# Kurtosis of 1024 rows on one core: a first load in two pieces, three groups loaded as whole rows, and dummy matmuls before the first transposes

## The chip, the cores and the metric

The kernel runs on one core of one Trainium2 chip. The metric is the device time in microseconds (us) of one execution; lower is better. Times are given as the median of several executions with the lowest and the highest. The profile's span is some 1.8 us shorter than the time (95.2 us against 97.0 us for the kernel before), and all moments below are counted from the start of the span.

## The reference

```
def reference(x):                       # x: 1024 x 8192, float32
    mean = np.mean(x, axis=-1, keepdims=True)
    std = np.std(x, axis=-1, keepdims=True)
    z = (x - mean) / (std + 1e-8)
    return (np.mean(z ** 4, axis=-1) - 3).astype(np.float32)
```

The input is 33.55 MB and is read once. Each row needs its mean first, then the sum of squares and the sum of fourth powers of the centred values.

## The kernel before

The 1024 rows are worked through in 16 groups of 64 rows. A row lies on two partitions, so that a group is a tile of 128 partitions and 4096 columns. Five such tiles are held at a time. For each group the list says in which pieces its columns are loaded, how many columns of the fourth power ScalarE takes (VectorE takes the rest), and which engine forms the mean.

```
GROUPS = [
    (2, [4096], 1280, 'DVE'),
    ...
    (2, [4096], 1536, 'DVE'),               # group 3
    (2, [2304, 1792], 640, 'PE'),           # group 4, the first with transposes
    ...
    (2, [1536, 1280, 768, 512], 1760, 'both'),   # group 15
]
```

All loads go through one queue, one transfer for a piece:

```
def load(i):
    ...
    for w in pieces:
        nc.sync.dma_start(out=xt[:, c:c + w], in_=src[:, c:c + w])
        c += w
```

Groups 0 to 3 get their mean from one VectorE instruction that adds the two halves of the whole tile, and a matmul. Groups 4 to 14 get it from 32 transposes on TensorE that add up in PSUM (`tps`), a reduction on VectorE (`red`) and a matmul (`mps`). ScalarE copies the result (`nmu`) and squares the tile with it as bias:

```
def mean(i):
    if engine == "DVE":
        nc.tensor.matmul(mps, lhsT=blk[k], rhs=added_halves(i, 0), start=True, stop=True)
    ...
    else:
        tps = transposed_sums(i, n_cols // k)        # 32 transposes of 128 x 128
        nc.tensor.matmul(mps, lhsT=pair_sums(tps), rhs=negcol, start=True, stop=True)
    nc.scalar.copy(nmu, mps)

def keep_busy(n):                                    # the dummies; used at the tail already
    for _ in range(n):
        nc.tensor.matmul(idle, lhsT=zeros[:, :P], rhs=zeros, start=True, stop=True)

for i in range(L):
    mean(i)
    square(i)                                        # ScalarE
    if i >= 1:
        fourth_dve(i - 1, GROUPS[i - 1][2])          # VectorE
        load_next(i - 1)                             # the tile of group i-1 is free
    ...
    fourth_act(i, 0, GROUPS[i][2])                   # ScalarE
```

## Time and profile before

| | before |
|---|---|
| time, 6 runs | 97.08 us (97.00 to 97.14) |
| span of the profile | 95.2 us |
| busy: TensorE, VectorE, ScalarE | 62%, 76%, 84% |
| DMA, mean over the span | 353 GB/s, 433 GB/s from 10 to 15 us |
| first load: issued, wanted data there | 0.80, 8.6 us |

The busy shares say little here, since they are averages. What counts are the two rows of digits in which hardly a slice is below 9 (ScalarE and DMA), and the places where one of the two is seen to wait for the other. The prediction shows these lines.

### The profile page before, as it was taken

To read this page: it belongs to the slowest core of one execution; us is meant where nothing else is said; L and a number is where in the kernel's file an instruction comes from. 1 tells how busy PE (TensorE), PEld (TensorE's weight loads), DVE (VectorE), ACT (ScalarE), POOL (GpSimd) and SP (SyncE) were. 2 spreads that over 40 slices of the span, in tenths; PEclk is the share of its full clock that TensorE was granted. 3 is DMA by queue.
4 is the path that set the end of the run, shared out by engine and by line. 5 is a ranking of instruction groups with operands and counts; after the bars stand their busy time and mean duration, and the time that the engine had idled before them with its cause. 6 is when DMAs were issued, how large, how long until landed. Compare 5 with 4: busy or idle time off the path is not lost.

```text
span 95.2 us, 1248 instructions
## 1 busy us (share of the span) xinstructions
PE 59.5 (62%) x450; PEld 52.5 (55%) x450; DVE 72.7 (76%) x63; ACT 79.8 (84%) x88; POOL 2.7 (3%) x12
## 2 busy tenths in 40 slices
PE   0000202001089797979796969797979797989770
PEld 0000202001089696969695959686969696874330
DVE  2003529999995294979797979897999698999970
ACT  6000099999999779999999999999999999999970
POOL 6400000000000000000000000000000000000000
PEclk9999999999999999999999999999999999999999
DMA  4799999999999999999999999999999999700000
GB/s 89 268 433 433 433 427 433 440 433 394 425 429 413 425 428 429 412 422 412 433 409 430 424 419 420 415 408 403 423 412 420 416 407 408 276 15 0 0 0 1
DMA packets 4789, 33.63 MB, mean 353 GB/s; under 512 B 560, under 2 KB 560, under 8 KB 3248
## 3 DMA queue, kind: packets, MB, share of 16 engines
q1 hardware_dynamic: 4784, 33.56, 85.6%
q8 instruction: 3, 0.05, 0.2%
q14 instruction: 2, 0.02, 0.1%
HBM read 33.55 MB, written 0.00 MB: 352 GB/s over the span
## 4 chain that ended last, share of the span: by engine, by line
PE 26%; DMA 24%; ACT 18%; DVE 18%; issue 11%; SPq 0%; DVEq 0%
DMA xt<-in_x_dram 24%; PE tps L138 21%; ACT xt L182 16%; DVE xt L194 7%; DVE junk L155 7%; DVE red L144 2%; PE mps L174 2%; ACT xt L189 1%; PE pk L240 1%; PE mps L165 1%; PE pf L232 1%; SPq L132 0%; ACT nmu L176 0%; DVE q L194 0%; PE p L222 0%
## 5 line engine op out<-in xcount | busy, mean ns | idle before, releaser
L182 ACT ACTIVATE xt<-xt,nmu 128x4096 f32<-128x4096 f32 (+1 forms) x17 | 59.8, 3516 | 0.5
L194 DVE CUSTOM_DVE_ANT_0 xt<-xt 128x3456 f32<-128x3456 f32 (+8 forms) x17 | 57.5, 3386 | 2.3 <-ACT xt L182 1.9
L138 PE MATMUL tps<-ident,xt 128*128 128x128 f32 x380 | 46.9, 282 | 0.5 <-DMA xt<-in_x_dram 0.5
L138 PEld LDWEIGHTS tps<-ident,xt 128*128 128x128 f32 x380 | 43.9, 147 | 1.8 <-DMA xt<-in_x_dram 0.9
L165 PE MATMUL mps<-part,blk 128*128 128x1 f32 x8 | 2.3, 351 | 24.8 <-DVE part L155 24.8
L155 DVE CUSTOM_DVE_ANT_0 junk<-xt 128x2048 bf16<-128x2048 f32 (+1 forms) x5 | 9.6, 1915 | 9.9 <-DMA xt<-in_x_dram 9.9
L165 PEld LDWEIGHTS mps<-part,blk 128*128 128x128 f32 x8 | 2.0, 311 | 25.0 <-issue 11.0
L189 ACT ACTIVATE xt<-xt 128x640 f32<-128x640 f32 (+7 forms) x16 | 13.9, 870 | 0.5
L176 ACT COPY nmu<-mps 128x1 f32<-128x1 f32 x16 | 2.4, 148 | 10.7 <-PE mps L165 9.4
L144 DVE TENSOR_REDUCE red<-tps 128x128 f32<-128x256 f32 x12 | 5.1, 424 | 6.7 <-PE tps L138 6.6
L174 PEld LDWEIGHTS mps<-negcol,red 128*128 128x128 f32 x22 | 3.3, 188 | 8.9 <-issue 3.3
L174 PE MATMUL mps<-negcol,red 128*128 128x1 f32 x22 | 3.9, 249 | 6.5 <-DVE red L144 5.3
L203 PE MATMUL idle<-zeros 128*128 128x512 f32 x10 | 4.8, 609 | 0.0
L182 ACT ACTIVATION_READ_ACCUMULATOR xt<-xt,nmu 128x1 f32 x17 | 3.1, 184 | 0.0
L189 ACT ACTIVATION_READ_ACCUMULATOR xt<-xt 128x1 f32 x16 | 3.0, 186 | 0.0
L203 PEld LDWEIGHTS idle<-zeros 128*128 128x128 f32 x10 | 1.7, 191 | 1.4 <-issue 1.4
L67 ACT ACT_TABLE_LOAD x1 | 1.3, 1283 | 0.8 <-PEq L301 0.8
L194 DVE DVE_READ_ACCUMULATOR2_ANT q<- 128x1 f32 x17 | 1.4, 83 | 0.0
L218 PEld LDWEIGHTS p<-s,blk 128*128 128x128 f32 x4 | 0.7, 189 | 1.2 <-ACT xt L182 0.7
L66 DVE MEMSET zeros<- 128x512 f32 x1 | 0.5, 485 | 1.0 <-PEq L301 1.0
L218 PE MATMUL p<-s,blk 128*128 128x1 f32 x4 | 0.7, 234 | 0.7 <-ACT xt L182 0.7
L240 PE MATMUL pk<-blk,q 128*5 128x64 f32 (+1 forms) x10 | 1.0, 219 | 0.0
(32 smaller groups left out, 10.5 us busy)
## 6 DMA issues: line engine op xcount, KB each, us to landing
xt<-in_x_dram SPq DMA_DIRECT2D x8, 1152.0 KB, 11.4
xt<-in_x_dram SPq DMA_DIRECT2D x4, 2048.0 KB, 14.5
xt<-in_x_dram SPq DMA_DIRECT2D x8, 896.0 KB, 13.3
xt<-in_x_dram SPq DMA_DIRECT2D x7, 768.0 KB, 11.1
xt<-in_x_dram SPq DMA_DIRECT2D x3, 512.0 KB, 12.5
xt<-in_x_dram SPq DMA_DIRECT2D x1, 640.0 KB, 12.0
xt<-in_x_dram SPq DMA_DIRECT2D x1, 384.0 KB, 12.4
xt<-in_x_dram SPq DMA_DIRECT2D x1, 256.0 KB, 11.3
```

Source lines behind the costliest of these rows:

```text
L138: nc.tensor.matmul(tps, lhsT=xts[i][:, c:c + P], rhs=ident, start=c == 0, stop=c == w - P, is_transpose=True)
L144: nc.vector.tensor_reduce(out=red.rearrange("p (r k) -> p r k", k=2), in_=tps.rearrange("p (r k) -> p r k", k=2).unsqueeze(2).to_broadcast ...
L155: nc.vector.tensor_tensor_reduce(out=junk[:, :h], in0=t[:, :h], in1=t[:, h:], scale=1.0, scalar=0.0, op0=AO.add, op1=AO.add, accum_out=part)
L165: nc.tensor.matmul(mps, lhsT=blk[k], rhs=added_halves(i, 0), start=True, stop=True)
L174: nc.tensor.matmul(mps, lhsT=pair_sums(tps), rhs=negcol, start=True, stop=True)
L176: nc.scalar.copy(nmu, mps)
L182: nc.scalar.activation(out=t, in_=t, func=AF.Square, bias=nmus[i], accum_out=s2[:, j + second:j + second + 1])
L189: nc.scalar.activation(out=t, in_=t, func=AF.Square, accum_out=quads[0][:, j:j + 1])
L194: nc.vector.tensor_tensor_reduce(out=t, in0=t, in1=t, scale=1.0, scalar=0.0, op0=AO.mult, op1=AO.add, accum_out=quads[1 + second][:, j:j + 1])
L203: nc.tensor.matmul(idle, lhsT=zeros[:, :P], rhs=zeros, start=True, stop=True)
L218: nc.tensor.matmul(p2[:, n - 1:], lhsT=blk[k], rhs=s2[:, n - 1 + j:n + j], start=j == 0, stop=j == 1)
L240: nc.tensor.matmul(pk, lhsT=t, rhs=m, start=j == 0, stop=j == len(terms) - 1)
```

## The change

Its intent, as the few words given with it and the code let one read it: fewer transfers for the groups whose columns need not be there early, the clock of TensorE raised before the first transposes so that they take 3.7 and not 5.9 us, and a first load whose first part is small. The columns of ScalarE for groups 4 to 7 are lowered to go with it.

```
 GROUPS = [
-    (2, [4096], 1280, 'DVE'),
+    (2, [1024, 3072], 1280, 'DVE'),
     ...
-    (2, [2304, 1792], 640, 'PE'),      # groups 4, 5, 6: three such lines
+    (2, [4096], 576, 'PE'),
-    (2, [2304, 1792], 640, 'PE'),      # group 7
+    (2, [2304, 1792], 512, 'PE'),
 ...
+    FIRST = [g[3] for g in GROUPS].index("PE")      # 4
     ...
     for i in range(L):
+        if i == FIRST - 1:
+            keep_busy(4)
         mean(i)
```

More of the change, by code (lines that the diff above doesn't have):

```diff
@@ L20 @@
     (2, [4096], 1536, 'DVE'),
-    (2, [2304, 1792], 640, 'PE'),
-    (2, [2304, 1792], 640, 'PE'),
-    (2, [2304, 1792], 640, 'PE'),
-    (2, [2304, 1792], 640, 'PE'),
+    (2, [4096], 576, 'PE'),
+    (2, [4096], 576, 'PE'),
+    (2, [4096], 576, 'PE'),
+    (2, [2304, 1792], 512, 'PE'),
     (2, [2304, 1792], 512, 'PE'),
```

## The prediction

> **What bounds the kernel now.** I read the page first (busy shares, the slices, the chain), then the timeline from 8 us to the end, then the waits, then the busy time in short stretches. The slices come first; each digit is a fortieth of the 95.2 us span, 2.38 us.
>
> ```profile
> ACT  6000099999999779999999999999999999999970
> ...
> PEclk9999999999999999999999999999999999999999
> DMA  4799999999999999999999999999999999700000
> GB/s 89 268 433 433 433 427 433 440 433 394 425 429 413 425 428 429 412 422 412 433 409 430 424 419 420 415 408 403 423 412 420 416 407 408 276 15 0 0 0 1
> ```
>
> The reader is to see two resources without slack. The DMA engines are full from slice 3 to slice 34, and ScalarE from slice 6 on, with one dip in slices 14 and 15 (31 to 36 us). PEclk shows only what the throttle grants. It does not show whether TensorE has warmed up.
>
> The dip is explained by the timeline from 21 to 34 us (start, duration, engine, line, operation, in brackets the idle time before it and who ended it):
>
> ```profile
> 21.30 0.56 PE L165 MATMUL mps<-part,blk 128*128 128x1 f32 x2 [4.73 <-DVE part L155]
> ...
> 26.53 0.56 PE L165 MATMUL mps<-part,blk 128*128 128x1 f32 x2 [4.67 <-DVE part L155]
> ...
> 26.95 5.87 PE L138 MATMUL tps<-ident,xt 128*128 128x128 f32 x32
> ...
> 27.12 0.16 ACT L176 COPY nmu<-mps 128x1 f32<-128x1 f32 x1
> ...
> 32.85 0.42 DVE L144 TENSOR_REDUCE red<-tps 128x128 f32<-128x256 f32 x1 [2.92 <-PE tps L138]
> ...
> 33.64 3.69 PE L138 MATMUL tps<-ident,xt 128*128 128x128 f32 x32
> 33.81 0.16 ACT L176 COPY nmu<-mps 128x1 f32<-128x1 f32 x1 [1.09 <-PE mps L174]
> ```
>
> The first 32 transposes (group 4) take 5.87 us, the next 32 (group 5) 3.69 us. ScalarE needs the mean of group 4 and waits 1.09 us for it. That is its only long idle time after it starts. The stretches of 0.25 us (length, busy and number of transposes that begin, clock granted, DMA share, GB/s) show the first set going slowly, then fast:
>
> ```profile
> 29.00:29.25 0.25, 0.25 (x3) 1.00 1.07 442
> ...
> 31.75:32.00 0.25, 0.25 (x5) 1.00 1.03 430
> ```
>
> What carries from there to the end is in the timeline at 64 to 67 us, group 11:
>
> ```profile
> 64.18 1.51 PEld L138 LDWEIGHTS tps<-ident,xt 128*128 128x128 f32 x14 [0.15 <-DMA xt<-in_x_dram]
> ...
> 65.97 0.42 DVE L144 TENSOR_REDUCE red<-tps 128x128 f32<-128x256 f32 x1 [0.57 <-PE tps L138]
> ...
> 66.54 0.35 PE L174 MATMUL mps<-negcol,red 128*128 128x1 f32 x2 [0.61 <-DVE red L144]
> 66.68 0.19 ACT L189 ACTIVATION_READ_ACCUMULATOR xt<-xt 128x1 f32 x1
> ...
> 66.93 0.16 ACT L176 COPY nmu<-mps 128x1 f32<-128x1 f32 x1
> ```
>
> The second piece of group 11 arrives at 64.18 and TensorE is waiting for it. Its mean is ready at 66.89, and ScalarE is free at 66.87. **Two chains meet here to within 0.02 us**: arrivals through TensorE, and ScalarE's own work since 33.81. From here TensorE's chain of transposes, reduction and mean goes on at about 4.8 us a group to the mean of group 14 (ready at 81.37, ScalarE free at 81.29), and the tail of some 11 us is fixed. So a gain on only one of the chains is lost at group 11. The end moves by roughly the smaller of the two gains.
>
> **What the Trainium skill says.** "TensorE: Matmul & The Clock Gate", Part 1 (the HAM clock gate): the array runs at half clock until one activity window of about 3.4 us has been busy, and the window runs freely, so the moment depends on its phase. The trace agrees: TensorE becomes busy at 26.53 and speeds up at about 31.5, 5 us later. The same page, Part 4 (PE-mode transpose), says that transposes do not count as busy in the same way, so that full clock is not reached. This trace differs: the speed changes in the middle of nothing but transposes. "DMA: Bandwidth & Descriptors", section Bandwidth, puts the fabric ceiling at 435 GB/s. The trace agrees with 433 GB/s in the stretch from 10 to 15 us, where each row goes as one packet, and has 421 from 30 to 40 us, where a row goes in two.
>
> **The change part by part.**
>
> *Whole rows for groups 4 to 6.* A group is 128 x 4096 x 4 bytes, 2.10 MB: at 433 GB/s 4.84 us, at 421 GB/s 4.98 us. Each transfer saved is thus worth about 0.1 to 0.14 us of DMA time. Three are saved, 0.3 to 0.4 us. The price is that transposes of a group wait for all of it. Group 1 landed at 13.49; with three more groups at about 4.86, group 4 lands whole near 28.0, group 5 near 33, group 6 near 37.9. Before, their transposes began at 26.95, 33.64 and 38.15. So only group 4's must begin later, by about 1 us, and once TensorE is warm that is harmless: 28.1 + 3.7 + 0.05 + 0.44 + 0.14 + 0.37 puts its mean at 32.8, a microsecond before the 33.8 of now.
>
> *First group in two pieces.* The mean of group 0 is one VectorE instruction over halves of the whole row, so nothing can use the first 1024 columns early. The extra transfer costs 0.1 to 0.14 us. The ramp of the queue may change: in slices 1 and 2 it moves 89 and 268 GB/s, and the first load lands 7.8 us after issue, of which 4.84 us is transfer. Smaller first packets could shorten the ramp or lengthen it; I see nothing in the trace that decides, and set it to 0 with an uncertainty of 0.3 us. Net of DMA: 3 less 1 is two transfers, about **0.25 us gained**.
>
> *Columns moved from ScalarE to VectorE.* Groups 4 to 6 lose 64 columns each, group 7 128, 320 in all. ScalarE takes 0.74 us for 640 columns and 0.63 for 512, so 0.86 ns a column: **0.27 us** off ScalarE. VectorE takes it up where it has waits of 0.3 to 0.6 us a group.
>
> *Four dummy matmuls ahead of the mean of group 3.* In the tail the same call is this line:
>
> ```profile
> 85.82 3.68 PE L203 MATMUL idle<-zeros 128*128 128x512 f32 x8
> ```
>
> Eight records for four calls, 0.43 us from one weight load to the next, so 3.44 us warm and twice that, 6.9 us, cold. They begin when the mean of group 2 is done, 21.86. If the clock rises w after that, they end at 21.86 + w + (6.9 - w)/2. The mean of group 3 stands behind them in TensorE's queue and has its operand at 26.53. For w = 3.0 they end at 26.8, for 4.9 (what the transposes show now) at 27.8, for 6.4 at 28.5. The mean is then about 0.2 us shorter than its cold 0.56. ScalarE, free for it at 27.18, thus loses about 0.1, 1.0 or 1.8 us. In return the 1.09 us wait at 33.81 goes. **Net on ScalarE +1.0, +0.1 or -0.7 us**, to which the 0.27 is added.
>
> *Sum.* DMA chain +0.25 us. ScalarE chain +0.4 us in the middle case. The smaller counts: about 0.25 us off, 97.04 to **96.8 us**.
>
> **The rivals.** (a) *The dummies become the wait that they remove.* If the window falls badly, the mean of group 3 comes 2 us late and ScalarE is 0.4 us behind even with its fewer columns. For it speaks that 6.9 us of cold work goes into a gap of 4.7 us. Against it, ScalarE has about 0.2 us of slack between groups 11 and 14. The time would be 97.0 to 97.4. (b) *The cold start was the real bound, and all of the 1.09 us is got back.* The chain of waits, followed back from the end, indeed passes through these transposes. Against it stand the arrivals at 49.3 to 64.2, for which TensorE waits whatever ScalarE does; only the pairing with a faster ramp, of 0.5 us or more, would let it through: 96.0 to 96.4. (c) *All hidden:* the ramp of the first group eats the two saved transfers: 97.0.
>
> **Range and chances.** The middle case 96.8, rival (a) about one in four, (c) one in five, (b) one in eight. Eight times in ten 96.3 to 97.3. Two per cent is 1.94 us, which is more than the sum of everything that I find on either side: faster 0.04, same 0.94, slower 0.02.
>
> **What would show each step.** Right: group 4's 32 transposes at about 3.7 us, beginning near 28; no wait of ScalarE at the mean of group 4 but one of up to 1 us at that of group 3; group 1 landing within 0.3 us of 13.49; group 11's last piece about 0.2 us before 64.18; ScalarE at most level with TensorE there. Wrong: group 0 landing 0.5 us or more away from 8.6, which would mean that the ramp depends on the first piece; the dummies ending after 28.5; the first transposes still slow; or the arrival of group 11 moving by 0.5 us or more, in which case the price of a transfer was mis-sized.

## The result, and the profile after

| | before | after |
|---|---|---|
| time, 6 runs each, same rounds | 97.08 us (97.00 to 97.14) | 97.43 us (96.92 to 97.52) |
| ratio of after to before | | 1.0027, 95% interval 1.0006 to 1.0048 |
| after once more, on another occasion (5 runs; before 11 runs) | 97.07 us (96.95 to 97.18) | 97.11 us (96.98 to 97.28) |
| ratio | | 1.0008, 95% interval 0.9996 to 1.0020 |

A ratio is the mean time of one kernel's runs over that of the other's of the same rounds, so it is not quite the ratio of the medians. The change gained nothing. It is slower by 0.3% the first time and the same the second time. The predicted 0.25 us did not come, and the 97.43 us lies above the range.

The slices of the page after, which answer to the first fence of the prediction (a slice is 2.39 us):

```profile
ACT  6000099999959999999999999999899999899980
...
DMA  1999999999999999999999999999999999500000
GB/s 43 285 427 460 418 425 432 432 432 439 439 418 432 439 432 385 427 425 406 424 420 428 424 418 421 408 408 415 419 409 428 406 417 402 218 17 0 0 0 1
```

ScalarE's dip has moved from slices 14 and 15 to slice 12, from the mean of group 4 to that of group 3. The first slice of the queue is thinner: 43 instead of 89 GB/s.

The timeline after, from the first VectorE instruction (which waits for the whole of group 0) to the mean of group 5; columns as in the prediction:

```profile
9.11 2.29 DVE L155 CUSTOM_DVE_ANT_0 junk<-xt 128x2048 bf16<-128x2048 f32 x1 [7.66 <-DMA xt<-in_x_dram]
...
21.66 0.56 PE L165 MATMUL mps<-part,blk 128*128 128x1 f32 x2 [4.73 <-DVE part L155]
...
22.08 6.36 PE L203 MATMUL idle<-zeros 128*128 128x512 f32 x8
...
28.28 0.28 PE L165 MATMUL mps<-part,blk 128*128 128x1 f32 x2
...
28.59 0.16 ACT L176 COPY nmu<-mps 128x1 f32<-128x1 f32 x1 [0.93 <-PE mps L165]
...
28.60 3.71 PE L138 MATMUL tps<-ident,xt 128*128 128x128 f32 x32
...
33.58 3.69 PE L138 MATMUL tps<-ident,xt 128*128 128x128 f32 x32 [0.30 <-DMA xt<-in_x_dram]
...
34.11 0.14 ACT L176 COPY nmu<-mps 128x1 f32<-128x1 f32 x1
```

The first transposes now take 3.71 us, not 5.87. In exchange the dummies hold TensorE until 28.44, so ScalarE waits 0.93 us for the mean of group 3, where before it waited 1.09 us for that of group 4. And the first line begins at 9.11. In the kernel before the same line reads:

```profile
8.63 2.29 DVE L155 CUSTOM_DVE_ANT_0 junk<-xt 128x2048 bf16<-128x2048 f32 x1 [7.17 <-DMA xt<-in_x_dram]
```

Group 0 is there **0.48 us later** than before, and since everything starts from it, ScalarE and the arrivals are both late from the beginning. At group 11, where the two chains meet:

```profile
64.54 1.51 PEld L138 LDWEIGHTS tps<-ident,xt 128*128 128x128 f32 x14 [0.31 <-DMA xt<-in_x_dram]
...
66.90 0.35 PE L174 MATMUL mps<-negcol,red 128*128 128x1 f32 x2 [0.61 <-DVE red L144]
...
67.29 0.16 ACT L176 COPY nmu<-mps 128x1 f32<-128x1 f32 x1 [0.35 <-PE mps L174]
```

The second piece arrives 0.36 us later than before (64.54 against 64.18), and ScalarE waits 0.35 us for the mean. So the arrivals set the end here. The last instruction of the chain, the product L242, begins 0.45 us later than before; 0.36 us of this was there at group 11. First the kernel before, then after:

```profile
92.90 0.21 DVE L242 TENSOR_TENSOR kr<-pk,frow 5x64 f32<-5x64 f32 x1 [0.48 <-PE pk L240]
```

```profile
93.35 0.21 DVE L242 TENSOR_TENSOR kr<-pk,frow 5x64 f32<-5x64 f32 x1 [0.47 <-PE pk L240]
```

The profiled run of the kernel before took 96.96 us, less than any of its six timed runs, and that of the kernel after 97.42 us. So the profiles lie further apart than the times.

The trace also records when each of the 16 DMA engines finished its share of each transfer. These records are not a view of the page. I read from them, for the last piece of a group, when the engine in the middle (the median of the 16) and the last engine were done (us):

```
kernel                         group 0      group 1      group 3      group 6      group 7      group 11
before                       8.21/ 8.61  13.08/13.49  22.88/23.29  37.78/38.20  42.77/44.28  62.67/64.14
after                        8.35/ 8.97  13.25/13.86  23.04/23.66  37.72/38.34  42.69/44.48  62.62/64.50
after, again (e12)           8.39/ 9.03  13.30/13.93  23.08/23.72  37.77/38.40  42.73/44.67  62.80/64.53
e1  first group in one       8.20/ 8.56  13.08/13.44  22.88/23.22  37.56/37.90  42.53/44.20  62.40/64.09
e3  split of group 0 only    8.29/ 9.12  13.19/14.02  22.99/23.82  37.89/38.78  42.85/44.61  62.88/64.59
e6  3072 first, group 0      8.55/ 8.88  13.45/13.77  23.23/23.56  38.16/38.48  43.12/44.75  63.07/64.69
e9  1024/3072, group 1       8.13/ 8.55  13.48/14.37  23.25/24.17  38.17/39.09  43.15/44.62  63.05/64.51
e10 2304/1792, group 1       8.10/ 8.70  13.18/13.93  22.98/23.72  37.88/38.64  42.85/43.61  62.74/64.33
e13 1280/2816, group 1       8.16/ 8.58  13.17/13.71  22.95/23.50  37.87/38.43  42.84/44.47  62.73/64.66
e14 2048/2048, group 1       8.09/ 8.62  13.06/13.57  22.84/23.37  37.75/38.29  42.73/44.27  62.63/64.41
e11 1024/3072, group 3       8.09/ 8.70  12.98/13.56  23.33/24.43  38.23/39.33  43.20/44.79  63.10/64.99
```

A group can be used when the last engine is done. Single profiles differ, so I also took all of them together. Group 0 loaded whole (eleven profiles) is done at 8.09 to 8.21 on the middle engine and at 8.55 to 8.82 on the last one; with 1024 columns first (after, e12, e2, e3) at 8.29 to 8.39 and 8.97 to 9.12. The means are 0.21 and 0.39 us later. Group 11 is done on the last engine at 64.02 to 64.31 where groups 0 to 3 are whole (six profiles), and at 64.50 to 64.59 with the split. The lines of the experiments are read below.

### The profile page after: what moved, and what is told of

The parts are those of the page before. It is cut to its first block, busy times and chain, and to the rows that moved or that the text cites. A ratio compares the mean times of both kernels' runs of the same rounds, so it can differ in the third digit from the quotient of the medians.

```text
span 95.6 us, 1263 instructions
## 1 busy us (share of the span) xinstructions
PE 63.6 (67%) x458; PEld 52.7 (55%) x458; DVE 73.0 (76%) x63; ACT 79.5 (83%) x88; POOL 2.7 (3%) x12
## 4 chain that ended last, share of the span: by engine, by line
DMA 26%; PE 24%; ACT 22%; DVE 13%; issue 11%; SPq 1%; DVEq 0%
DMA xt<-in_x_dram 26%; ACT xt L182 20%; PE tps L138 13%; PE idle L203 7%; DVE xt L194 5%; DVE junk L155 5%; DVE red L144 2%; ACT xt L189 2%; PE mps L174 2%; PE pk L240 1%; SPq L132 1%; PE mps L165 1%; ACT nmu L176 1%; PE pf L232 1%; DVE q L194 0%
## 5 line engine op out<-in xcount | busy, mean ns | idle before, releaser
L194 DVE CUSTOM_DVE_ANT_0 xt<-xt 128x3584 f32<-128x3584 f32 (+9 forms) x17 | 57.8, 3406 | 1.7 <-ACT xt L182 1.6
L138 PE MATMUL tps<-ident,xt 128*128 128x128 f32 x380 | 44.8, 275 | 1.2 <-DMA xt<-in_x_dram 1.0
L138 PEld LDWEIGHTS tps<-ident,xt 128*128 128x128 f32 x380 | 41.4, 141 | 2.7 <-PE mps L174 1.0
L189 ACT ACTIVATE xt<-xt 128x512 f32<-128x512 f32 (+8 forms) x16 | 13.7, 853 | 0.5
L203 PE MATMUL idle<-zeros 128*128 128x512 f32 x18 | 11.1, 770 | 0.0
L203 PEld LDWEIGHTS idle<-zeros 128*128 128x128 f32 x18 | 4.2, 251 | 4.5 <-issue 4.5
L189 ACT ACTIVATION_READ_ACCUMULATOR xt<-xt 128x1 f32 x16 | 3.0, 186 | 0.0
(32 smaller groups left out, 10.5 us busy)
```

The source lines that it names most:

```text
L138: nc.tensor.matmul(tps, lhsT=xts[i][:, c:c + P], rhs=ident, start=c == 0, stop=c == w - P, is_transpose=True)
L189: nc.scalar.activation(out=t, in_=t, func=AF.Square, accum_out=quads[0][:, j:j + 1])
L194: nc.vector.tensor_tensor_reduce(out=t, in0=t, in1=t, scale=1.0, scalar=0.0, op0=AO.mult, op1=AO.add, accum_out=quads[1 + second][:, j:j + 1])
```

## The experiments

Theory T: the split of the first load delays every arrival, and this delay sets the end. Theory R: the dummies hold up the mean of group 3, and this sets the end. Each kernel has six runs beside the kernel before, one of them with the profile (e12 has five). All results were correct.

**e1, the changed kernel with the first group in one piece.**

```
-    (2, [1024, 3072], 1280, 'DVE'),
+    (2, [4096], 1280, 'DVE'),
```

> The changed kernel with the first group in one piece again, everything else kept. Theory T (the split first load arrives later, 8.97 against 8.61 us on its slowest engine, and that lag stays to the end): group 0 lands at 8.6 again, the last piece of group 11 at 64.0 to 64.2 instead of 64.5, and the time falls by 0.3 to 0.5 us, to 96.9 to 97.1. Theory R (the dummies hold up the mean of group 3 and ScalarE sets the end): the landings come back, the end does not; 97.4.

Measured: 97.11 us (96.99 to 97.27), ratio to before 1.0005 (0.9992 to 1.0018). In its profile the mean of group 3 and the last piece of group 11 read:

```profile
27.34 0.16 ACT L176 COPY nmu<-mps 128x1 f32<-128x1 f32 x1 [0.21 <-PE mps L165]
...
64.14 1.51 PEld L138 LDWEIGHTS tps<-ident,xt 128*128 128x128 f32 x14 [0.15 <-DMA xt<-in_x_dram]
```

Group 0 is there at 8.56 again, and group 11's piece is used at 64.14, 0.40 us earlier than in the changed kernel. The profiled end comes 0.51 us earlier (L242 at 92.84). This is what T expects. In the times it is less sure: 97.11 is below the first measurement of the changed kernel (97.43) and equal to the second (97.11). It also shows that the rest of the change, without the split, gains nothing on the kernel before.

**e3, the split alone** (the kernel before, with group 0 in `[1024, 3072]`).

> The kernel before, with only its first group in pieces of 1024 and 3072. Theory T: the landing of every group is 0.35 us (ramp) plus up to 0.1 us later, to group 11 at 64.5 to 64.6, and the time is 97.4 to 97.6. Theory R (the ramp has nothing to do with it): within 0.15 us of the kernel before, 97.0 to 97.2.

Measured: 97.74 us (97.34 to 97.86), ratio 1.0063 (1.0044 to 1.0081). Group 0 is there at 9.12 on its last engine and group 11 at 64.59, 0.45 us later than before:

```profile
64.63 1.51 PEld L138 LDWEIGHTS tps<-ident,xt 128*128 128x128 f32 x14 [0.27 <-DMA xt<-in_x_dram]
```

The cost of the split is clear here: 0.6 us by the ratio of the times, where the prediction had 0.1 to 0.14 us.

**e2, the changed kernel without the dummies** (the line `keep_busy(4)` in the loop is taken out).

> The changed kernel without its four dummy matmuls. Theory T: with whole rows the first transposes cannot begin before group 4 has landed, about 28.4, and are cold, 5.9 us; the mean of group 4 is then ready at about 35.3 and ScalarE comes 1.2 us later than in the changed kernel, which is more than its slack of 0.3 us at group 11; the time rises by 0.6 to 1.0 us, to 98.0 to 98.4. Theory R: the wait of 0.93 us at the mean of group 3 goes and the time falls by some 0.4 us, to 97.0.

Measured: 98.09 us (97.46 to 98.55), ratio 1.0098 (1.0063 to 1.0134). R falls: without the dummies the kernel is slower. The profile shows the transposes waiting for the whole row and then running cold, and ScalarE waiting for them:

```profile
28.66 6.17 PE L138 MATMUL tps<-ident,xt 128*128 128x128 f32 x32 [1.12 <-DMA xt<-in_x_dram]
...
35.83 0.16 ACT L176 COPY nmu<-mps 128x1 f32<-128x1 f32 x1 [2.60 <-PE mps L174]
```

**e5, whole rows alone** (the kernel before, groups 4 to 6 as `[4096]`, no dummies, columns as before).

> The kernel before, with only groups 4 to 6 as whole rows, columns unchanged, no dummies. My theory: the first transposes begin at 28.2, when all of group 4 is there, and are cold; the mean of group 4 is ready near 35 instead of 33.8; the 0.3 us that the transfers save cannot be used and ScalarE sets the end: 97.8 to 98.3, with a spread of 0.5 us or more between runs since the moment at which the clock rises varies. Rival (fewer transfers pay by themselves): 96.7 to 96.9.

Measured: 98.13 us (97.50 to 98.84), ratio 1.0106 (1.0066 to 1.0146). The middle engine finishes group 6 at 37.53, 0.25 us earlier than before. It was 0.03 us early at group 3 already, so the three transfers save 0.22 us, less than the 0.3 to 0.4 us that they were said to save. But ScalarE waits 2.91 us for the mean of group 4 in the profile, and the runs differ by 1.3 us among themselves. Whole rows need the dummies.

**e4, the dummies alone** (the kernel before, `keep_busy(4)` ahead of the mean of group 3).

> The kernel before, with only the four dummies ahead of the mean of group 3. Theory T: the dummies end near 28.3, ScalarE waits about 0.9 us at the mean of group 3 and not at that of group 4; the two cancel; 97.0 to 97.3. Theory R: the dummies cost what the change lost or more, 97.4 to 97.6.

Measured: 97.24 us (96.91 to 97.45), ratio 1.0016 (0.9999 to 1.0034). The wait of 0.83 us at group 3 takes the place of that at group 4. The two cancel, as expected.

**e8 and e7, six and three dummies** (both with the first group in one piece).

```
-            keep_busy(4)
+            keep_busy(6)        # e8; keep_busy(3) in e7
```

> The changed kernel with one first piece and six dummies instead of four: the last two run at full clock, 0.86 us each, and hold the mean of group 3 back by 1.7 us more. My theory: ScalarE had 0.2 to 0.3 us of slack at group 11 in the run with four, so the time rises by 1.2 to 1.5 us over that kernel, to 98.3 to 98.6. Rival (the arrivals set the end by a wide margin): 97.0 to 97.4.

Measured: 97.39 us (97.05 to 98.47), ratio 1.0051 (1.0009 to 1.0092). My expectation was wrong: ScalarE bears more than I said. In the profile, a run of 97.05 us:

```profile
28.77 0.16 ACT L176 COPY nmu<-mps 128x1 f32<-128x1 f32 x1 [1.54 <-PE mps L165]
...
34.28 0.14 ACT L176 COPY nmu<-mps 128x1 f32<-128x1 f32 x1
```

A wait of 1.54 us at group 3 puts the mean of group 4 at 34.28, 0.47 us later than in the kernel before. The 320 columns that ScalarE no longer has give back 0.27, and of the remaining 0.2 us nothing reaches the end: at group 11 ScalarE takes the mean at 66.94, 0.17 us after it is ready, and the last product begins at 92.77, 0.07 us before that of e1. So a mean of group 4 near 34.3 is about break-even. The run of 98.47 us was not profiled; that its clock rose later and held the mean back by more is an inference.

> The changed kernel with one first piece and three dummies instead of four: they end near 26.8 even when all are cold, so that the mean of group 3 is held back by 0.3 us at most. My theory: the arrivals set the end, 97.0 to 97.2, no better than four dummies, with rare runs up to 98 where the clock does not rise in time. Rival (the dummies' wait was costing): 96.6 to 96.8.

Measured: 97.20 us (96.81 to 97.38), ratio 1.0010 (0.9994 to 1.0026), no gain. The profiled run shows a failure that I had half expected:

```profile
28.31 5.37 PE L138 MATMUL tps<-ident,xt 128*128 128x128 f32 x32 [1.34 <-DMA xt<-in_x_dram]
```

By the trace's record of TensorE's clock, the clock rose at 24.92, fell at 28.33 and rose again at 31.75. The three dummies were over at 26.17, and TensorE then had one short matmul until the row came. The transposes therefore ran cold again. The fourth dummy bridges this gap: with four the clock does not fall before the transposes (after, e1, e4, e12).

**e6, the two pieces in the other order** (the kernel before, group 0 as `[3072, 1024]`), and **e9, the split on the second group** (group 1 as `[1024, 3072]`, group 0 whole).

> The kernel before, with only its first group in pieces of 3072 and 1024: the same two transfers in the other order. Theory S (small packets at the front of the ramp are what delays: each engine still has slow packets then, and a small one carries little): the first group lands within 0.15 us of 8.6, the time is 97.0 to 97.3. Theory X (any transfer more at the front costs, for its boundary on each engine): lands at 9.0 to 9.1 as with the small piece first, 97.5 to 97.8.

> The kernel before, with its second group, not its first, in pieces of 1024 and 3072, so that the extra boundary lies in the steady part of the queue. If the cost is that of the ramp: the second group lands 0.1 us later than 13.49, the time is 97.1 to 97.3. If a transfer more costs 0.4 us wherever it stands: lands at 13.9, 97.5 to 97.8.

Measured: e6 97.67 us (97.58 to 97.74), ratio 1.0060 (1.0042 to 1.0078); e9 97.65 us (97.42 to 98.10), ratio 1.0067 (1.0040 to 1.0094). Both cost as much as e3. So the order makes no difference, and the cost also comes where there is no ramp. In e9 the ramp is over, and the last engine finishes group 1 at 14.37 instead of 13.49. The stretch from 8 to 10.5 us (columns as in the prediction's stretches, with PEld, DVE, ACT and POOL between), before and then in e9:

```profile
8.00:10.50 2.50, 0.00 (x0) 0.00 (x0) 1.87 (x1) 0.00 (x0) 0.00 (x0) 1.00 0.99 426
```

```profile
8.00:10.50 2.50, 0.00 (x0) 0.00 (x0) 1.93 (x1) 0.00 (x0) 0.00 (x0) 1.00 1.06 372
```

The engines are full in both, 0.99 and 1.06, and move 372 instead of 426 GB/s. A part of the packets is slower. In e9's records the 128 packets of 4096 bytes of group 1 take 210 ns on average, the 384 packets of this size in the groups at the end of the kernel before take 163 ns. But 74 of the 128 took 159 ns; they begin from 7.4 to 8.6 us. The other 54 begin from 8.0 to 9.9 us and took up to 399 ns. In e6, where the 1024 columns come second, all 128 took 159 ns, and yet the middle engine finishes group 0 0.34 us later than before. So it is not the size of the packets alone.

**e10, e13, e14, other cuts of the second group; e11, the cut of the change on the fourth.** e10 is `[2304, 1792]`, e13 `[1280, 2816]`, e14 `[2048, 2048]`, all on group 1; e11 is `[1024, 3072]` on group 3.

> The kernel before, with only its second group in pieces of 2304 and 1792, the sizes that later groups have. If the sizes 1024 and 3072 are what is slow: the second group lands 0.1 us later than 13.49 and the time is 97.1 to 97.3. If any boundary among the first loads costs 0.4 us or more: lands at 13.9 to 14.4, 97.5 to 97.8.

> The kernel before, with only its fourth group in pieces of 1024 and 3072. It lands at 23.3 on its slowest engine and is not wanted before 24.1, so nothing waits for it directly. If the sizes are what is slow, the lag of 0.4 to 0.8 us stays in the queue to group 11 and the time is 97.4 to 97.8. If only the first ten us are sensitive: 0.1 us later, 97.1 to 97.3.

> The kernel before, with only its second group in pieces of 1280 and 2816 columns: rows of 5120 and 11264 bytes, the small piece nearly as small as 1024 but no multiple of 4096 bytes. If a small first piece is what is slow: the median engine finishes the second group 0.3 to 0.4 us later than 13.08, 97.4 to 97.7. If it is the cut at a multiple of 4096 bytes: 0.1 us later, 97.1 to 97.3.

> The kernel before, with only its second group in two halves of 2048: no small piece, but a cut at a multiple of 4096 bytes. If a small first piece is what is slow: 0.1 us later, 97.1 to 97.3. If it is the cut at a multiple of 4096 bytes: 0.3 to 0.5 us later on the median engine, 97.4 to 97.8.

| kernel | time | ratio to before | middle engine, from the group before the cut one to the cut one |
|---|---|---|---|
| before | 97.0 to 97.2 | 1 | 4.87 us (group 0 to 1) |
| e9, 1024/3072 | 97.65 | 1.0067 (1.0040 to 1.0094) | 5.35 us, +0.48 |
| e10, 2304/1792 | 97.22 | 1.0022 (1.0006 to 1.0039) | 5.08 us, +0.21 |
| e13, 1280/2816 | 97.33 | 1.0030 (1.0014 to 1.0046) | 5.01 us, +0.14 |
| e14, 2048/2048 | 97.14 | 1.0009 (0.9992 to 1.0026) | 4.97 us, +0.10 |
| e11, 1024/3072 on group 3 | 97.45 | 1.0037 (1.0016 to 1.0057) | +0.55 over groups 2 and 3 |

The last column is worked out from the records above, 13.08 less 8.21 for the first line. A further transfer costs 0.1 to 0.2 us here, near the 0.1 to 0.14 us of the prediction, but about 0.5 us when the cut is 1024/3072, on group 1 and on group 3 alike. The slow packets are most of that: an engine has 8 of the 128, and 8 times the excess of the mean over 159 ns is 0.41 us in e9 (210 ns) and 0.54 us in e11 (226 ns). The column is of the middle engine only. On the last engine e13 has group 11 at 64.66, as late as e9, and its time is up by 0.3 us.

Both theories of the last call fall in part: 1280 columns are nearly as small and cost 0.14 us, and 2048 columns lie on a multiple of 4096 bytes and cost 0.10. Nor is it the size alone, for the place in the queue matters too. Groups 12 to 14 end in a piece of 1024 columns, and in the kernel before they take 5.04 to 5.09 us each on the middle engine, with three transfers; groups 8 to 10 take 4.96 to 4.97 us with two. And the cut 2304/1792 costs 0.21 us on group 1 (e10), but on groups 4 to 6 only 0.07 us each (0.22 us for three, from e5; e1 gives the same). What makes the packets slow stays **open**.

**e12, the changed kernel once more.**

> The changed kernel once more, unaltered, beside the others of this call: 97.3 to 97.5 by every theory.

Measured: 97.11 us (96.98 to 97.28), lower than expected by every theory; the figures are in the table of the result. In its profile the clock rose at 25.1 (27.5 in the first profile), the dummies ended at 27.3, and ScalarE's mean of group 4 came at 33.36. The arrival of group 11 was the same, 64.53, and L242 began at 93.27, 0.37 us later than in the kernel before. But the profiled run is one of the two slowest of the five (97.28); no profile shows the runs near 97.0. Over both occasions the changed kernel's 11 runs have a mean of 97.25 us. Why the two sets differ by 0.3 us is not settled.

No version tried here beats the kernel before. The best, e1, is level with it.

## Why the prediction was wrong

**Where two chains meet.** This held. In the after profile I can add up both up to group 11. ScalarE: 0.48 later at the start, a wait of 0.93 in place of 1.09 (0.16 less), 0.27 fewer columns, sum 0.05 later; measured, it is free at 66.95 instead of 66.87, 0.08 later. Arrivals: 0.36 later. The later of the two decides, and the end moved by 0.45. By the same sums, without the split ScalarE would have been some 0.4 us early and the arrivals level, which is what e1 shows at the end: no gain.

**Whole rows.** "Three are saved, 0.3 to 0.4 us" was too much, and what was saved did not arrive. From group 3 to group 6 the middle engine takes 14.68 us in e1 and 14.90 in the kernel before, 0.22 us less. The last engine finishes group 6 at 37.90 instead of 38.20, but at group 11 only 0.05 us are left (64.09 against 64.14). The other kernels with whole rows and no split have group 11 at 64.31, 64.17 and 64.02 (e5, e7, e8), and e4, without whole rows, has it at 64.04: no gain. Between groups 6 and 7 the last engine falls behind the middle one: by 0.42 before and 1.51 after in the kernel before, by 0.34 and 1.67 in e1. The third part of the page of the kernel before has the clue, the second queue in its list (packets, MB, share of the engines):

```profile
q1 hardware_dynamic: 4784, 33.56, 85.6%
q8 instruction: 3, 0.05, 0.2%
```

These three packets are fetches of instructions, 16 KB each. The records put the first at 41.76 us in the kernel before, where it takes 1.10 us on one engine. In e2 and e5 it comes at 43.8 and 43.7, after group 7 has landed, and there group 7 shows no such jump (0.69 and 0.64 us behind the middle engine) but group 8 does, 1.69 and 1.46 us. So the jump follows the fetch, and a gain of 0.2 us on the middle engine can be lost on the last one. No run moved the fetch by itself, so this is argued from the records and not shown; why the last engine loses more with whole rows is open.

**The first group in two pieces: this is the step that failed.** The prediction had "The extra transfer costs 0.1 to 0.14 us" and a ramp set "to 0 with an uncertainty of 0.3 us". It measured 0.36 us on the last engine in the changed kernel and 0.51 in e3, and 0.48 us at the first instruction that waits for it. The prediction counted DMA time, which is a mean over the engines. On the middle engine that was not far off: 0.14 us, and 0.21 over all profiles. But the group can be used only when the last engine is done, and this one was 0.39 us later over all profiles. The price was also taken from other pieces further down the queue (2304 and 1792 columns), and the cut 1024/3072 costs more than these (e9, e11). The cost comes without a ramp too; whether the ramp adds to it in group 0 is not shown. I had also counted the split against the arrivals alone. It delays ScalarE as much, since the whole kernel starts from group 0, so the rule of the smaller gain could not soften it.

**The sum of the DMA chain.** At group 11 the last engine was to be about 0.25 us early and was 0.36 us late, 0.61 us apart. The split makes up 0.3 of this: 64.50 less 64.09 (e1) is 0.41 us, where 0.1 to 0.14 was expected. The whole rows make up the other 0.3: a gain of 0.05 us and not of 0.3 to 0.4. So taking the split out does not bring the predicted gain (e1). Two of the signs named for being right also failed: group 1 landed 0.37 us after 13.49, and group 11's last piece was used 0.36 us after 64.18 and not 0.2 before it.

**Columns moved.** Right in size (the 16 instructions of L189 take 853 ns on average and not 870, 0.27 us in all), and used up: they are a part of why ScalarE was not the later chain.

**The dummies.** The formula held. The clock rose at 27.5, 5.4 us after the dummies began at 22.08, which gives an end at 22.08 + 5.4 + (6.9 - 5.4)/2 = 28.2; measured 28.44. The wait that they make, 0.93 us, fits the middle case of 1.0 by luck. The dummies ended near the third case (28.5, a wait of 1.8 us), but ScalarE itself was 0.48 us late, and it took the mean 0.15 us after their end, where the prediction allowed some 0.4. In e12 the clock rose 2.9 us after their start and they ended at 27.3, near the first case. Without them the changed kernel is 1% slower than the kernel before (e2).

**The rivals.** Rival (a) all but named the time, 97.0 to 97.4, with the wrong cause: the dummies did take the place of the wait, but e2 shows that beside whole rows they pay for themselves. Rival (c), the ramp eating the saved transfers, was nearest to what happened, and I had given it one chance in five. It was the loss in the first load, larger than in (c). Rival (b) fell.

## What to carry to other kernels

Before a load is cut, ask which instruction can use its first part; if none can, the cut is a cost only, and at the first load it delays every chain at once. Take the price of a cut from the same pieces at the same place in the queue: here 2304/1792 cost 0.07 us a group in groups 4 to 6 and 0.21 us on group 1, and 1024/3072 on group 1 cost about 0.5 us. Read an arrival from the last of the 16 DMA engines, not from their mean. A warm-up placed ahead of work on the path should last until that work begins and no longer; three dummies left a gap in which the clock fell, six held the path up.

## What the Trainium skill lacked or had wrong

- "DMA: Bandwidth & Descriptors", Specifications, gives 512 bytes as the least transfer for line rate. Of the packets of 4096 bytes at the head of a load of 1024 and 3072 columns in e9, 74 took 159 ns and 54 up to 399 ns (mean 210; in the last groups 163); the load took 0.48 us longer, with a head of 5120 bytes only 0.14. I found no page that has this.
- The same page, Queues, rings and completion order, names a queue row for the runtime's own use. Neither it nor "Runtime: NRT & Kernel Launch", where Instruction fetch mechanics describes the fetch, says what the fetch of instructions costs the loads. In the kernel before, after a 16 KB packet of 1.10 us at 41.76 us, the last engine's share of each load comes 1.5 us after the middle one's, where it had been 0.4 us, up to group 14.
- "TensorE: Matmul & The Clock Gate", Part 4, says that transposes do not bring full clock. In the kernel before the clock rose at 31.42, after 4.5 us in which it did nothing but transposes; 32 of them then took 3.69 instead of 5.87 us.
- The same page, Part 1, speaks of a busy window without saying how busy. By the recorded steps (3.41 us apart or multiples of it) a window of which TensorE was busy 2.43 us, 71%, did not raise the clock (after, 20.67 to 24.09); one that was busy throughout, 21.51 to 24.92, did (e7, busy from 21.39).
